# Up projection, quarters 1 to 3: both parts of h2 in one matmul of 512 columns

## The chip, the cores and the metric

The kernel runs on one core of one Trainium2 chip, in one launch. The metric is the device time of the kernel in microseconds (us). The kernel before takes 674.77 us, the median of 3 runs (674.47 to 674.83).

## What is computed

A decoder block on 512 tokens of width 1024 in float32. The part that the change touches is the MLP at its end:

```python
h2 = rmsnorm(x, norm_mlp_g[l])
z = jnp.square(jax.nn.relu(h2 @ w_up[l]))       # 1024 -> 4096
x = x + (z @ w_down[l]).astype(x.dtype)         # 4096 -> 1024
```

Ahead of it come a norm, one input projection, differential attention in 8 heads, a causal pooling in 4 groups, a gated merge and the output projection; after it, a final norm.

## The kernel before

Float32 products are made of three passes of the type fp32r: each operand x is split into a high part (a cast to fp32r) and a low part (x minus the high part), and high by high, high by low and low by high are added up in PSUM. The cast runs on ScalarE (`split_w`, L112), the subtraction on VectorE (L113).

The MLP goes in four quarters of 1024 hidden columns: `up(q)`, then `down(q)` (L975 to L979). Each is a multiplication of 2 by 2 blocks done with seven products in place of eight (Strassen's scheme in Winograd's form). The seven forms are named A11, A12, A22, S1, S2, S3, S4. For h2 they are made once, before quarter 0 (`forms_h2` and L655 to L662), and lie in the tiles `gab` and `gss` (L547 to L551): for each form the high part, then the low part, each of 4 k-tiles by 256 tokens (HS). Each quarter of w_up and of w_down has its seven forms made on the way by `weights` (L671): block b11 is loaded and cast; block sums are made by VectorE (L718) or by DMAs that add to what is in SBUF (L686, on POOL's queue); `parts` (L688) then splits each into wh and wl. Raw blocks b11 and b22 share two buffers (tag wr), b21 has one of its own, and wh and wl have room for three forms at a time, two in one pool and every third in another. The loads of raw blocks are on SP's queue (L681).

In `up`, `product` (L771) multiplies one form. Its output is 512 hidden rows (i = 0, 1 and p = 0, 1, 128 rows each) by 256 tokens. For one (i, p), it runs eight matmuls of 256 columns, high weights by the high (L782) and by the low part of h2 (L785), alternating over four k, and then four, low weights by the high part (L788): 12 matmuls. The two p of one i share a PSUM bank, so that a product has two banks of 512 columns. Twelve matmuls by four groups make 48 matmuls a product. `acc` hands out the banks 4, 5, 6, 7, 0, 1 in turn (L665); banks 2 and 3 (`m2`) belong to `down`.

In quarters 1 to 3, `up` goes in this order:

- A11 into the banks `ma`, copied to R[0] by ScalarE (`keep`, L810);
- S1 into the banks `mc`, copied to R[2];
- S2 onto `ma` (added in PSUM), copied to R[1];
- S3 onto `ma`, added to R[2] by VectorE (`join`, L814); ReLU and square of R[2] (`z_of`, L820, L821);
- A22 onto `ma`; ReLU straight out of the banks into R[3], and square;
- A12 into two banks of its own, joined to R[0] (`first_block`, L829), ReLU, square;
- S4 onto `mc`, joined to R[1].

From R, `sub` (L763, L765) makes the forms of z on VectorE and `zsplit` (L749) splits them (L752 ScalarE, L755 VectorE) for `down`. In `down`, the products (L865) have matmuls of 512 columns, in threes (L875, L877, L878), and VectorE adds the banks onto x1 (L895).

The order of the work on each engine is worked out when the kernel is built: a scheduler takes the instructions as their inputs come ready by its own estimate, and may put matmuls of one product between those of another. `after(later, earlier)` (L57) makes it place one instruction behind another; between two engines it adds no wait on the chip. The casts of the weights' forms are placed by such rules (`hold` in `parts`). Buffers and banks that are used again wait for their last reader.

Of the kernel before, what the change touches and what calls it, by code (L numbers as in the profile page):

```python
# [51 lines left out]
def block_kernel(ctx, tc, xT, x_tok, gains, pos, consts, w_in, w_v, w_pool, w_out, w_up, w_dn, out):  # L52
# [478 lines left out]
    HS = S // 2  # L531
# [12 lines left out]
    h2f = zf("h2f", F32)  # L544


    gab = [big.tile([P, j, 2, 4, HS], F32R, tag=t_, name=f"gab{j}") for j, t_ in ((1, "s1a"), (2, "s4"))]  # L547
    gss = [big.tile([P, 2, 2, 4, HS], F32R, tag=f"s{i}", name=f"gss{i}") for i in (2, 3)]
    gf = {}
    for form, g_, j in ((A11, gab[0], 0), (A12, gab[1], 0), (A22, gab[1], 1), (S1, gss[0], 0), (S2, gss[0], 1), (S3, gss[1], 0), (S4, gss[1], 1)):  # L550
        gf[form] = (g_[:, j, 0], g_[:, j, 1])  # L551
    rawz = bk.tile([P, 5, 4, HS], F32, name="rawz")
    R = [rawz[:, i] for i in range(5)]
    st = cp.tile([P, NT, 8], F32, name="st2")
# [36 lines left out]
    def forms_h2(forms, x):  # L591

        w, u, a11, a12 = (h_[:, i, :, x] for h_ in (hw, h2f) for i in range(2))
        for form in forms:
            ins = None
            if form in (S2, S4):
                ins = V.scalar_tensor_tensor(out=w, in0=w, scalar=-1.0, in1=a11 if form == S2 else a12, op0=ALU.mult, op1=ALU.subtract)
            elif form == S3:
                ins = V.tensor_tensor(out=u, in0=a11, in1=u, op=ALU.subtract)
            if form in (S3, S4):  # L600
                after(ins, state[form - 1])
            hi, lo = (g_[:, :, x] for g_ in gf[form])
            A.copy(out=hi, in_=u if form == S3 else w)
            state[form] = V.tensor_tensor(out=lo, in0=u if form == S3 else w, in1=f(hi), op=ALU.subtract)

# [20 lines left out]
    for t in range(NT):  # L626
        a_ = bank(4 + t, f"po1_{t}")
        for k in range(NK):
            m, end = mm_rows(a_, t, k, ws[k // 2], k == 0, k == NK - 1)
            if t > 1 and k == 0:  # L630
                after(m, state["po"])
        if 0 < t < 3:
            for b in range(2):
                after(state["h2T", t - 1, b], end)
        state["po"] = end
        x1_add(t, 1, a_)
        V.scalar_tensor_tensor(out=h2[:, t % 2], in0=x1[:, t, :], scalar=row_scale(t, 1), in1=g2b, op0=ALU.mult, op1=ALU.mult)
        pv = []
        for b in range(2):
            pt = bank((t % 2) * 2 + b, f"h2T{t}_{b}")  # L640
            for j in range(4):
                k = 4 * b + j
                if j == 1:
                    state["h2T", t, b] = state["h2T"]
                state["h2T"] = T.transpose(out=pt[:, j * P : j * P + P], in_=h2[:, t % 2, k * P : k * P + P], identity=ident)
            pv.append(pt.rearrange("p (j q) -> p j q", q=P))
        sl = slice((t % 2) * P, (t % 2) * P + P)
        if t > 1:

            A.copy(out=hw[:, 1, :, sl], in_=pv[0])  # L650
            V.tensor_tensor(out=hw[:, 0, :, sl], in0=pv[1], in1=hw[:, 1, :, sl], op=ALU.subtract)
            forms_h2((S1, S2), sl)
        if t == 3:
            forms_h2((S3,), slice(0, HS))
        for b in range(t // 2, 2):  # L655
            hi, lo = (gab[b][:, t // 2, i, :, sl] for i in range(2))
            A.copy(out=hi, in_=pv[b])
            part = V.tensor_tensor(out=lo, in0=pv[b], in1=f(hi), op=ALU.subtract)
            if t == 3:
                after(part, state[S3])  # L660
            if t < 2:
                A.copy(out=h2f[:, b, :, sl], in_=pv[b])  # L662
# [8 lines left out]
    def weights(src, q, nm, order):  # L671
# [16 lines left out]
        def parts(rs, b, hold=None, add=None):  # L688

            third = nparts[0] % 3 == 2  # L690
            nparts[0] += 1
            out_ = []
            for c in range(2):
                hi, lo = (
                    (bk if third else wp).tile([P, 1024], F32R, tag=t_ + "b" * third, name=f"{t_}_{nm}{b}_{q}_{c}", bufs=2 if third else 4)
                    for t_ in ("wh", "wl")
                )
                if add is None:
                    cast = split_w(rs[c], hi, lo, eng=V)
                else:  # L700

                    cast = A.copy(out=hi, in_=rs[c])
                    A.mul(out=lo, in_=f(hi), mul=-1.0)
                    G.dma_start(out=lo, in_=src[q, add, c], accum_op=ALU.add)
                if hold:
                    after(cast, hold)
                if early and b == f"t{A22}":
                    after(cast, state["keep"])
                out_.append((hi, lo))
            return out_  # L710

# [31 lines left out]
    def halves(r):  # L743
        return [r[:, 2 * i : 2 * i + 2, :] for i in range(2)]

    def bank_view(pa):
        return [pa[i].rearrange("p (a t) -> p a t", a=2) for i in range(2)]

    def zsplit(q, form, r):  # L749

# [16 lines left out]
    def up(q):  # L767

        W = weights(w_up, q, "u", (A11, A12, S1, S2, S3, A22, S4) if q == 0 else (A11, S1, S2, S3, A22, A12, S4))

        def product(form, name, onto=None):  # L771
            w, pa = next(W), onto or [acc(f"u{name}{q}_{i}") for i in range(2)]
            rh, rl = gf[form]
            first.append(None)
            for i in range(2):
                hi, lo = w[i]
                for p in range(2):
                    begin = None
                    a_ = pa[i][:, p * HS : p * HS + HS]
                    for k in range(4):  # L780
                        c = slice((p * 4 + k) * P, (p * 4 + k) * P + P)
                        m = T.matmul(a_, lhsT=hi[:, c], rhs=rh[:, k, :], start=p + k == 0 and onto is None, stop=False, skip_group_check=True)  # L782
                        first[-1] = first[-1] or m
                        begin = begin or m
                        T.matmul(a_, lhsT=hi[:, c], rhs=rl[:, k, :], start=False, stop=False, skip_group_check=True)  # L785
                    for k in range(4):
                        c = slice((p * 4 + k) * P, (p * 4 + k) * P + P)
                        m = T.matmul(a_, lhsT=lo[:, c], rhs=rh[:, k, :], start=False, stop=k == 3, skip_group_check=True)  # L788
                        if q == 0 and form == A12 and (i, p, k) == (1, 0, 0):
                            after(m, state["h2T"])  # L790
                    if q == 0:
                        if (form, i, p) == (A11, 0, 1):
                            for b in range(2):
                                after(state["h2T", 2, b], m)
                        elif (form, i, p) == (A11, 1, 1):
                            for b in range(2):
                                after(state["h2T", 3, b], m)
                        if form != A11 or i + p:
                            after(begin, state["um"])
                        state["um"] = m  # L800

            if form == A22:
                state["m4"] = m
            elif form == S4:
                after(first[-1], state["m4"])
            return pa

        def keep(pa, r):
            for a_, r_ in zip(bank_view(pa), halves(r)):
                state["keep"] = A.copy(out=r_, in_=a_)  # L810

        def join(pa, r, hold=None):
            for a_, r_ in zip(bank_view(pa), halves(r)):
                state["join"] = V.tensor_tensor(out=r_, in0=a_, in1=r_, op=ALU.add)  # L814
                if hold:
                    after(state["join"], hold)

        def z_of(r, sign, pa=None):
            for i, r_ in enumerate(halves(r)):
                A.activation(out=r_, in_=bank_view(pa)[i] if pa else r_, func=AF.Relu, scale=sign)  # L820
                ins = A.activation(out=r_, in_=r_, func=AF.Square)  # L821
            return ins

        ma = product(A11, "m1")
        keep(ma, R[0])
        if q == 0:
            forms_h2((S4,), slice(0, HS))
# [8 lines left out]
            first_block()  # L836
        mc = product(S1, "m5")
        keep(mc, R[2])
        product(S2, "m6", onto=ma)
        keep(ma, R[1])  # L840
        product(S3, "m7", onto=ma)
        join(ma, R[2])
        state["joined"] = state["join"]
        z_of(R[2], -1.0)
        product(A22, "m4", onto=ma)
        if q == 0:
            zsplit(q, A11, R[0])
        zhi["z21"] = z_of(R[3], 1.0, ma)
# [183 lines left out]
```

## Time and profile before

| what | value |
|---|---|
| median of 3 runs | 674.77 us (674.47 to 674.83) |
| the profiled execution's own time | 674.09 us |
| its span, first to last instruction | 671.9 us |
| around the span | 2.2 us |
| mean granted clock of TensorE | 0.996 |
| VectorE busy | 526.1 us (78%) |
| ScalarE busy | 461.0 us (69%) |
| up, quarters 1 to 3, with the down product that runs into it | 423.6 to 469.4, 502.1 to 547.9, 580.5 to 626.3 us |

PE is TensorE, PEld its weight loads, DVE VectorE, ACT ScalarE, POOL GpSimd, SP the engine whose queue issues most loads. A matmul's duration in the profile (283 ns at 256 columns, 389 ns at 512) is that of the whole pipeline; the time that one more matmul costs is the distance between the starts of two. A row of waits reads: who waited, for whom, us in total, times, longest. A row of the timeline reads: start and duration in us, engine, line, operation, output<-inputs, form, count, and in brackets how long the engine had been idle and what ended it. A row of a group reads: busy us, mean ns | idle us before it, and what ended that. A row of windows gives, for a stretch, the busy time (and count) of PE, PEld, DVE, ACT and POOL, the granted clock, the share of DMA and GB/s.

### The profile page before, as it was taken

The page shows a single profiled execution, that of the slowest core. Times are in us where ns is not written, and L with a number is a line of the kernel's source. Part 1 is how long each engine was busy: PE and PEld are TensorE (multiplying, and loading weights), DVE is VectorE, ACT ScalarE, POOL GpSimd, SP SyncE. Part 2 cuts the span into 40 slices and gives each one's busy share as a digit, 9 for nine tenths or more (in the row PEclk, how much of TensorE's full clock was granted, in tenths as well). Part 3 has the DMA queues.
Part 4 walks back from the last instruction along what each step waited for, and adds up shares of the span by engine and source line. Part 5 has one row for each costly group of instructions (what it writes and reads, how often), then busy time and mean ns, then how long its engine had stood idle before and what let it go on. Part 6 is the DMA issues. An engine that isn't in the chain of part 4 may idle for free.

```text
span 671.9 us, 9994 instructions
## 1 busy us (share of the span) xinstructions
PE 663.1 (99%) x3688; PEld 579.6 (86%) x3688; DVE 526.1 (78%) x882; ACT 461.0 (69%) x741; POOL 112.0 (17%) x130
## 2 busy tenths in 40 slices
PE   9999999999999999999999999999999999999995
PEld 7888888888888888888889988999889998899884
DVE  6855977799979986875588998657994599747995
ACT  8465587978887698884477975367743695256974
POOL 2001110142133212520202020202102021210120
PEclk9999999999999999999999999999999999999998
DMA  9416464435263365574976596776959578494863
GB/s 317 162 57 185 126 151 126 103 94 126 87 142 103 98 166 105 126 184 172 312 208 112 159 235 186 167 191 146 236 199 187 193 164 261 117 212 132 214 126 125
DMA packets 32880, 109.34 MB, mean 163 GB/s; under 512 B 4032, under 2 KB 4928, under 8 KB 32832
## 3 DMA queue, kind: packets, MB, share of 16 engines
q0 software_dynamic: 10656, 38.80, 32.3%
q1 hardware_dynamic: 21744, 69.38, 29.3%
q8 instruction: 29, 0.48, 0.3%
q10 hardware_dynamic: 432, 0.52, 0.2%
q14 instruction: 19, 0.16, 0.1%
HBM read 106.59 MB, written 2.10 MB: 162 GB/s over the span
## 4 chain that ended last, share of the span: by engine, by line
PE 98%; DMA 1%; DVE 0%; ACT 0%; issue 0%; SPq 0%
PE um L785 8%; PE um L788 8%; PE um L782 8%; PE dm L875 8%; PE dm L877 8%; PE dm L878 8%; PE v L235 2%; PE o L418 2%; PE ga L132 2%; PE ga L131 2%; PE gp L135 2%; PE gp L132 2%; PE k L132 2%; PE k L131 2%; PE gp L131 2%; PE k L135 2%
## 5 line engine op out<-in xcount | busy, mean ns | idle before, releaser
L877 PE MATMUL dm<-wh_dt,z 128*128 128x512 f32 (+1 forms) x128 | 49.5, 386 | 0.0
L878 PE MATMUL dm<-wl_dt,z 128*128 128x512 f32 (+1 forms) x128 | 49.4, 386 | 0.0
L875 PE MATMUL dm<-wh_dt,z 128*128 128x512 f32 (+1 forms) x128 | 49.0, 387 | 0.0
L785 PE MATMUL um<-gss,wh_ut 128*128 128x256 f32 x192 | 48.2, 283 | 0.0
L782 PE MATMUL um<-gss,wh_ut 128*128 128x256 f32 x192 | 48.0, 283 | 0.0
L401 ACT ACTIVATE p<-p,st 128x128 f32<-128x128 f32 (+3 forms) x64 | 35.7, 558 | 14.1 <-DVE st L397 13.8
L895 DVE TENSOR_TENSOR x<-x,dm 128x512 f32<-128x512 f32 x48 | 32.5, 681 | 16.3 <-PE dm L878 16.3
L112 ACT CAST wh_ut<-wga_uNone 128x1024 fp32r<-128x1024 f32 x24 | 24.9, 1050 | 29.7 <-PE dm L877 19.2
L112 ACT CAST wh_ub<-wr_u 128x1024 fp32r<-128x1024 f32 x24 | 25.1, 1050 | 22.1 <-PE um L785 9.8
L686 POOL DMA_DIRECT2D wga_dNone<-w_dn x16 | 14.2, 885 | 154.2 <-DVE wl_dt L113 154.2
L113 DVE TENSOR_TENSOR wl_ut<-wga_uNone,wh_ut 128x1024 fp32r<-128x1024 f32 x24 | 29.1, 1221 | 13.0 <-ACT wh_ut L112 12.9
L877 PE MATMUL dm<-wh_db,z 128*128 128x512 f32 x96 | 37.2, 389 | 0.0
L878 PE MATMUL dm<-wl_db,z 128*128 128x512 f32 x96 | 37.2, 389 | 0.0
L785 PEld LDWEIGHTS um<-gss,wh_ut 128*128 128x128 f32 x192 | 36.9, 192 | 0.0
L782 PEld LDWEIGHTS um<-gss,wh_ut 128*128 128x128 f32 x192 | 36.8, 192 | 0.0
L875 PE MATMUL dm<-wh_db,z 128*128 128x512 f32 x96 | 35.7, 389 | 0.0
L113 DVE TENSOR_TENSOR wl_ub<-wr_u,wh_ub 128x1024 fp32r<-128x1024 f32 x24 | 29.1, 1219 | 7.4 <-ACT wh_ub L112 7.4
L686 POOL DMA_DIRECT2D wga_uNone<-w_up x18 | 15.6, 865 | 115.8 <-DVE wl_ut L113 81.4
L112 ACT CAST wh_dt<-wga_dNone 128x1024 fp32r<-128x1024 f32 x24 | 24.9, 1049 | 14.4 <-issue 6.7
L755 DVE TENSOR_TENSOR z<-rawz,z 128x1024 fp32r<-128x1024 f32 x28 | 33.6, 1218 | 0.5 <-ACT z L752 0.5
L397 DVE CUSTOM_DVE_ANT_0 p<-s,mask 128x128 f32<-128x128 f32 (+3 forms) x64 | 30.3, 484 | 3.6 <-PE s L396 3.5
L785 PE MATMUL um<-gab,wh_ub 128*128 128x256 f32 x128 | 32.5, 283 | 0.0
(324 smaller groups left out, 2203.3 us busy)
## 6 DMA issues: line engine op xcount, KB each, us to landing
wr_u<-w_up SPq DMA_DIRECT2D x24, 512.0 KB, 5.4
wr_d<-w_dn SPq DMA_DIRECT2D x24, 512.0 KB, 4.2
wga_uNone<-w_up POOLq DMA_DIRECT2D x18, 512.0 KB, 7.2
wga_dNone<-w_dn POOLq DMA_DIRECT2D x16, 512.0 KB, 5.7
wr_k<-w_in SPq DMA_DIRECT2D x8, 512.0 KB, 3.3
wr_ga<-w_in SPq DMA_DIRECT2D x8, 512.0 KB, 3.3
wr_gp<-w_in SPq DMA_DIRECT2D x8, 512.0 KB, 4.2
wl_ga<-w_in POOLq DMA_DIRECT2D x8, 512.0 KB, 5.4
```

Of the source, the lines that this page charges most:

```text
L112: ins = A.copy(out=hi[:, sl], in_=raw[:, sl])
L113: (eng or G).tensor_tensor(out=lo[:, sl], in0=raw[:, sl], in1=f(hi)[:, sl], op=ALU.subtract)
L131: T.matmul(acc, lhsT=hi[:, c], rhs=rh[:, k, :], start=k == 0, stop=False)
L132: T.matmul(acc, lhsT=hi[:, c], rhs=rl[k], start=False, stop=False)
L401: A.activation(out=pr[:, c, :N], in_=pr[:, c, :N], func=AF.Exp, scale=-1.0, bias=st[:, c : c + 1], accum_out=st[:, 2 + c : 3 + c])
L755: lo = V.tensor_tensor(out=z[:, 1], in0=r, in1=f(z[:, 0]), op=ALU.subtract)
L782: m = T.matmul(a_, lhsT=hi[:, c], rhs=rh[:, k, :], start=p + k == 0 and onto is None, stop=False, skip_group_check=True)
L785: T.matmul(a_, lhsT=hi[:, c], rhs=rl[:, k, :], start=False, stop=False, skip_group_check=True)
L788: m = T.matmul(a_, lhsT=lo[:, c], rhs=rh[:, k, :], start=False, stop=k == 3, skip_group_check=True)
L875: m = T.matmul(a_, lhsT=zh, rhs=hi[:, sl], start=p == 0 and start, stop=False, skip_group_check=True)
L877: T.matmul(a_, lhsT=zl, rhs=hi[:, sl], start=False, stop=False, skip_group_check=True)
L878: end = T.matmul(a_, lhsT=zh, rhs=lo[:, sl], start=False, stop=p == 3, skip_group_check=True)
```

## The change

The tiles `gab` and `gss` are laid out so that, for each k, the high and the low part of h2 lie next to each other. In quarters 1 to 3 the products A11, S2, S3 and A22 are wide: each (i, p) has a bank of its own, and for each k one matmul of 512 columns streams both parts under the high weights, so that the first half of the bank gathers high by high and the second half high by low. The four low-weight matmuls of 256 columns go onto the first half. S1, S4 and A12 stay as they were, as does quarter 0.

`ma` then has four banks. Its two halves are added after the bank: `keep` copies the second half to R by ScalarE and VectorE adds the first; `join` adds both halves to R, one after the other, by VectorE; A22 goes through `keep` before its ReLU, which reads R. The banks are handed out by a list for each quarter: x and y to A11, z to S1, x again to A12, and in `down` y and x.

The casts of form A22 in quarters 1 to 3 are placed behind ScalarE's copies of S2's banks. In quarter 3 the second cast of A22 is placed behind S3's second join, those of block b21 (form A12) behind S3's sixth join and A22's first add, and those of b22 (form S4) behind A22's second add.

```diff
-    gab = [big.tile([P, j, 2, 4, HS], F32R, tag=t_, name=f"gab{j}") for j, t_ in ((1, "s1a"), (2, "s4"))]
-    gss = [big.tile([P, 2, 2, 4, HS], F32R, tag=f"s{i}", name=f"gss{i}") for i in (2, 3)]
+    gab = [big.tile([P, j, 4, 2, HS], F32R, tag=t_, name=f"gab{j}") for j, t_ in ((1, "s1a"), (2, "s4"))]
+    gss = [big.tile([P, 2, 4, 2, HS], F32R, tag=f"s{i}", name=f"gss{i}") for i in (2, 3)]
...
-        gf[form] = (g_[:, j, 0], g_[:, j, 1])
+        gf[form] = (g_[:, j, :, 0], g_[:, j, :, 1], g_[:, j])
...
-                if early and b == f"t{A22}":
-                    after(cast, state["keep"])
+                if b == f"t{A22}" and nm == "u":
+                    after(cast, state["keep"] if early else state["kept", 2 * c + 1])
+                if nm == "u" and q == 3:
+                    if b == f"t{A22}" and c == 1:
+                        after(cast, state["joins"][1])
+                    elif b == "b21":
+                        after(cast, state["added"][0] if c else state["joins"][5])
+                    elif b == "b22":
+                        after(cast, state["added"][1])
...
+    def split_view(b_):
+        return b_.rearrange("p (a t) -> p a t", a=2)
...
-        def product(form, name, onto=None):
-            w, pa = next(W), onto or [acc(f"u{name}{q}_{i}") for i in range(2)]
-            rh, rl = gf[form]
+        def product(form, name, onto=None, wide=False):
+            w, pa = next(W), onto or [acc(f"u{name}{q}_{i}") for i in range(4 if wide else 2)]
+            rh, rl, both = gf[form]
...
-                    a_ = pa[i][:, p * HS : p * HS + HS]
+                    if wide:
+                        ab = pa[2 * i + p]
+                        a_ = ab[:, :HS]
+                    else:
+                        a_ = pa[i][:, p * HS : p * HS + HS]
                     for k in range(4):
                         c = slice((p * 4 + k) * P, (p * 4 + k) * P + P)
+                        if wide:
+                            m = T.matmul(ab, lhsT=hi[:, c], rhs=both[:, k].rearrange("p a t -> p (a t)"), start=k == 0 and onto is None, stop=False, skip_group_check=True)
+                            first[-1] = first[-1] or m
+                            continue
...
         def keep(pa, r):
+            if len(pa) == 4:
+                state["added"] = []
+                for i, ab in enumerate(map(split_view, pa)):
+                    state["kept", i] = A.copy(out=r[:, i, :], in_=ab[:, 1])
+                    state["added"].append(V.tensor_tensor(out=r[:, i, :], in0=ab[:, 0], in1=r[:, i, :], op=ALU.add))
+                return
...
         def join(pa, r, hold=None):
+            if len(pa) == 4:
+                state["joins"] = []
+                for i, ab in enumerate(map(split_view, pa)):
+                    for j in range(2):
+                        state["joins"].append(V.tensor_tensor(out=r[:, i, :], in0=ab[:, j], in1=r[:, i, :], op=ALU.add))
+                return
...
         def z_of(r, sign, pa=None):
+            if pa and len(pa) == 4:
+                keep(pa, r)
+                pa = None
...
-        ma = product(A11, "m1")
+        wide = q > 0
+        if wide:
+            x, y, z = ((0, 1), (6, 7), (4, 5)) if q % 2 else ((4, 5), (6, 7), (0, 1))
+            acc.ids, acc.n = x + y + z + x + y + x + z, 0
+        ma = product(A11, "m1", wide=wide)
...
-        product(S2, "m6", onto=ma)
+        product(S2, "m6", onto=ma, wide=wide)
         keep(ma, R[1])
-        product(S3, "m7", onto=ma)
+        product(S3, "m7", onto=ma, wide=wide)
...
-        product(A22, "m4", onto=ma)
+        product(A22, "m4", onto=ma, wide=wide)
```

More of the change, by code (lines that the diff above doesn't have):

```diff
@@ L601, in forms_h2 @@
                 after(ins, state[form - 1])
-            hi, lo = (g_[:, :, x] for g_ in gf[form])
+            hi, lo = (g_[:, :, x] for g_ in gf[form][:2])
             A.copy(out=hi, in_=u if form == S3 else w)
@@ L655, in block_kernel @@
         for b in range(t // 2, 2):
-            hi, lo = (gab[b][:, t // 2, i, :, sl] for i in range(2))
+            hi, lo = (gab[b][:, t // 2, :, i, sl] for i in range(2))
             A.copy(out=hi, in_=pv[b])
@@ L744, in halves @@
         return [r[:, 2 * i : 2 * i + 2, :] for i in range(2)]
+    def split_view(b_):
+        return b_.rearrange("p (a t) -> p a t", a=2)
     def bank_view(pa):
-        return [pa[i].rearrange("p (a t) -> p a t", a=2) for i in range(2)]
+        return [split_view(pa[i]) for i in range(2)]
     def zsplit(q, form, r):
```

## The prediction

> **What bounds the kernel now.** I read the page first, then the waits of TensorE, then the chain of waits in two short windows for the pace of single matmuls, then VectorE and ScalarE by stretch, and last the timeline of the fourth quarter. The page:
>
> ```profile
> span 671.9 us, 9994 instructions
> PE 663.1 (99%) x3688; PEld 579.6 (86%) x3688; DVE 526.1 (78%) x882; ACT 461.0 (69%) x741; POOL 112.0 (17%) x130
> PE 98%; DMA 1%; DVE 0%; ACT 0%; issue 0%; SPq 0%
> ```
>
> The waits of TensorE over the whole run, all of them:
>
> ```profile
> PE warm L170 <- POOL eps L161: 1.1, 1, 1.1
> PE v L235 <- ACT wh_v L112: 0.5, 1, 0.5
> ```
>
> TensorE waits 1.6 us in all, before the first products; in the MLP it never waits. So time comes off only by giving TensorE less to do, and stays off only while VectorE, ScalarE and the loads keep ahead of it. The chain of waits in a window of the first up projection (start, us, piece), and in one of a down projection:
>
> ```profile
> 358.94 0.48 PE um L788 x4
> 359.42 0.12 PE um L782
> 359.54 0.12 PE um L785
> ...
> 360.38 0.48 PE um L788 x4
> ```
>
> ```profile
> 488.40 0.23 PE dm L878
> 488.63 0.68 PE dm L875 x3
> 489.31 0.23 PE dm L877
> ```
>
> A group of twelve 256-column matmuls, from one L788 piece to the next, takes 360.38 - 358.94 = 1.44 us: 120 ns each. Three 512-column matmuls take 0.68 us: 226.7 ns each, not 240. A second row, from the input projection, says the same (1.81 / 8 = 226 ns):
>
> ```profile
> 61.06 1.81 PE q L135 x8
> ```
>
> The 256 further columns cost 106.7 ns, so each matmul carries about 120 - 106.7 = 13.3 ns that do not depend on its width.
>
> **The change, part by part.** *TensorE.* In quarters 1 to 3 four of seven up products become wide: A11, S2, S3 and A22. A product has four groups (i, p). A group was 12 x 120 = 1440 ns. It becomes four 512-column matmuls with the high part of the weights, over both parts of h2, and four of 256 with the low part: 4 x 226.7 + 4 x 120 = 1387 ns, 53.3 ns less. With 3 x 4 x 4 = 48 groups that is 2.56 us; 192 matmuls and weight loads of 3688 go. No row has a 512-column um matmul or a 512 followed by a 256 in one group. The bounds are the two 256s it replaces (240 ns, gain nothing) and the dm row (226.7); I take the dm row, which has the same operand types and a new weight load at each matmul.
>
> The Trainium skill, "TensorE: Matmul & The Clock Gate", section "Wait — 56ns, not 53.3ns?", puts a warm matmul's fixed cost at about 2.5 ns, so that N columns take N / 2.4 GHz + 2.5 ns; an estimate from that page for the 192 matmuls saved is 0.48 us. The rows above disagree with it (13.3 ns), and the measurement decides.
>
> *Evacuation.* A wide bank holds the product with the high part of h2 in its first half and that with the low part in its second; they are added after the bank. Rows of before, by form:
>
> ```profile
> L814 DVE TENSOR_TENSOR rawz<-um,rawz 128x512 f32<-128x512 f32 x24 | 16.4, 685 | 7.3 <-PE um L788 7.3
> L935 DVE TENSOR_TENSOR x<-x,dm 128x256 f32<-128x256 f32 x1 | 0.4, 414 | 0.0
> L810 ACT COPY rawz<-um 128x512 f32<-128x512 f32 x24 | 14.0, 583 | 16.9 <-PE um L788 16.8
> L820 ACT ACTIVATE rawz<-um 128x512 f32<-128x512 f32 x8 | 4.7, 592 | 4.1 <-PE um L788 4.0
> L948 ACT ACTIVATE rawz<-x 128x256 f32<-128x256 f32 x2 | 0.8, 409 | 0.5 <-DVE x L945 0.5
> ```
>
> VectorE per quarter: A11, S2 and A22 gain four adds each (12 x 0.414 = 4.97 us); S3's join goes from two of 685 to eight of 414 ns (+1.94 us); together +6.9 us. ScalarE: a 256-column copy out of a bank has no row; it lies between half of L810 (0.29) and L948 (0.41). I take 0.37, nearer to L948, since halving columns does not halve these rows. Twelve copies are 4.4 us, less the four of 583 they replace: +2.1 us. A22's ReLU then reads SBUF, at about the same price. Busy time by stretch (columns PE, PEld, DVE, ACT, POOL):
>
> ```profile
> 502.00:513.00 11.00, 11.00 (x71) 9.98 (x71) 5.02 (x6) 3.75 (x4) 3.51 (x4) 1.00 0.89 188
> 513.00:524.00 11.00, 11.00 (x94) 11.00 (x94) 5.03 (x5) 5.99 (x8) 1.73 (x2) 1.00 0.97 226
> 524.00:538.00 14.00, 14.00 (x119) 14.00 (x118) 9.06 (x9) 9.32 (x13) 0.00 (x0) 1.00 0.48 163
> 603.00:617.00 14.00, 14.00 (x119) 14.00 (x118) 9.01 (x10) 9.85 (x13) 0.00 (x0) 1.00 0.45 159
> 617.00:626.00 9.00, 9.00 (x77) 9.00 (x77) 8.49 (x10) 7.53 (x11) 3.51 (x4) 1.00 0.60 119
> 626.00:649.00 23.00, 23.00 (x104) 19.09 (x104) 23.00 (x27) 20.93 (x26) 3.48 (x4) 1.00 0.86 186
> ```
>
> In quarter 2 VectorE idles 6.0 us in the stretch of A11, 6.0 in that of S1 and S2 and 4.9 in that of S3 and A22; A11's and S2's 1.66 us of adds each and the 3.6 us of S3 and A22 fit there. That idle time is the cover: without it the 6.9 us a quarter would stand behind TensorE. From 617 on VectorE has no room, so what slips past that point arrives late.
>
> *Banks.* S3 adds onto the banks that S2 left, so it waits for their copies and adds. Each bank ends a quarter product apart, 1.39 us, and is written again one product later, so copy and add have 3 x 1.39 = 4.16 us; they need 0.37 + 0.41 us and what stands ahead in two queues. For S3's join it is 0.83 us against the same 4.16. A12 now takes the first two banks of the wide four, so it cannot start before A22's are out. In before it filled in between the halves of S3:
>
> ```profile
> 607.96 0.28 PE L785 MATMUL um<-gab,wh_ub 128*128 128x256 f32 x1
> 608.08 0.28 PE L782 MATMUL um<-gss,wh_ut 128*128 128x256 f32 x1
> ```
>
> and the copy out of S2's second bank, on ScalarE:
>
> ```profile
> 605.46 0.58 ACT L810 COPY rawz<-um 128x512 f32<-128x512 f32 x1
> ```
>
> This filler goes. It covered little: the copy that S3's second half needs ended at 606.04, and sixteen A12 matmuls (1.92 us) brought TensorE to 608.08. What is late next is such a copy, held up behind weight casts on ScalarE; the change puts A22's casts behind the copies. I price this at nothing.
>
> *The fixed order of the last quarter.* The casts of A12 (b21) and S4 (b22) stand behind the joins and A22's adds. Behind them stand the second subtraction of each (VectorE), the release of the raw buffer, the loads of w_dn on SP's queue, and the add L718 that makes S1's down weights. VectorE, ending with the two z parts for down's A11 and A12, and where down's S1, A11 and A12 start on TensorE:
>
> ```profile
> 607.70 1.22 DVE L113 TENSOR_TENSOR wl_ub<-wr_u,wh_ub 128x1024 fp32r<-128x1024 f32 x1
> 611.77 1.22 DVE L113 TENSOR_TENSOR wl_ub<-wr_u,wh_ub 128x1024 fp32r<-128x1024 f32 x1
> 614.39 1.23 DVE L718 TENSOR_TENSOR wga_dNone<-wr_d,wal_d 128x1024 f32<-128x1024 f32 x1 [1.41 <-DMA wr_d<-w_dn]
> 616.65 1.23 DVE L718 TENSOR_TENSOR wga_dNone<-wr_d,wal_d 128x1024 f32<-128x1024 f32 x1 [1.04 <-DMA wr_d<-w_dn]
> 619.53 1.22 DVE L113 TENSOR_TENSOR wl_dt<-wga_dNone,wh_dt 128x1024 fp32r<-128x1024 f32 x1
> 628.74 1.22 DVE L755 TENSOR_TENSOR z<-rawz,z 128x1024 fp32r<-128x1024 f32 x1
> 634.48 2.35 DVE L755 TENSOR_TENSOR z<-rawz,z 128x1024 fp32r<-128x1024 f32 x2
> ```
>
> ```profile
> 626.32 0.63 PE L875 MATMUL dm<-wh_dt,z 128*128 128x512 f32 x2
> 631.78 0.62 PE L875 MATMUL dm<-wh_db,z 128*128 128x512 f32 x2
> 637.22 0.62 PE L875 MATMUL dm<-wh_db,z 128*128 128x512 f32 x2
> ```
>
> Count back from down's start, 626.32. S4 and A12 take 5.76 each, so A22 ends at 614.80 and its second bank at 612.02; copy and add make it 612.8. Two casts of 1.05 (row below) with two copies between end near 615.6, the last subtraction at 616.8 (in before at 612.99). The load then needs 616.65 - 612.99 = 3.66 us: 620.5. Add, cast and subtraction (1.22 + 1.05 + 1.22) end at 624.0.
>
> ```profile
> L112 ACT CAST wh_db<-wr_d 128x1024 fp32r<-128x1024 f32 x22 | 22.5, 1050 | 7.9 <-PE dm L877 5.9 <-DMA wr_d<-w_dn 1.0 <-PE um L785 1.0
> ```
>
> Needed at 626.32 plus six matmuls, 627.7: 3.7 us are left in place of 7.0 (619.53 + 1.22 = 620.75). But one or two L718 (1.13 us each at the pace of the rows) slip into the stretch where VectorE has no room, while z for A11 (ends 629.96) has 1.8 us to spare and z for A12 (first of the two, 635.7) 1.5 us. So 0 to 0.5 us may be lost here; below nothing it cannot go, as TensorE did not wait before. I take 0.2 us.
>
> *Rest.* Quarter 0 only reads and writes h2 at other strides, in runs no shorter than 128 elements; nothing. Quarters 1 and 2 have no fixed casts for b21 and b22.
>
> *Sum.* On the profiled execution's 674.09 us (span 671.9 and 2.2 around it): -2.56 + 0.2 = -2.36, so 671.7; from the median of 674.77, 672.4.
>
> **The rivals.** *B, VectorE late in quarter 3.* If both L718 wait for their load while the subtraction and z part behind them stand in the queue, the spare 1.5 us is overrun: two adds (2.3) and the two last adds of A22 (0.8), less 1.5 to spare, lose 1.6 us: 674.77 - 2.56 + 1.6 = 673.8. For it: L718 waited for a load in these rows already. Against: the loads may be issued in time for other work to go first.
>
> *C, slower.* One mechanism: L718 at the head of VectorE's queue, waiting for w_dn, in quarter 3. Behind the second one, done at 621.7, stand two joins (0.6 each at pace), two subtractions of weights (1.13 each), the difference R4 (1.13), its cast (1.05) and its low part (1.22): 628.6, 2.2 us after down's start. If that load takes as long as the first one did (608.92 to 614.39, 5.47 instead of 3.66) it is 4.0 us: 674.77 - 2.56 + 4.0 = 676.2. It decides from a wait of 2.56 us on. Against: it needs the worst order and the longer load.
>
> *D, the fixed cost doesn't go.* If the page's rule held for this pair of matmuls, or the low-part matmul after a wide one paid what the wide one saved, the gain would lie between 0 and 0.5 us: 674.3 to 674.8. The dm rows speak against.
>
> **How the numbers follow.** A measurement tells about 0.2% from no change, 1.35 us: faster is below 673.4, slower above 676.1. The forecast, 672.4 (its own range 671.9 to 673.0, the loss between 0 and 0.8), has 0.62; B 0.24 (673.0 to 674.6, a third of it below 673.4); D 0.05; C 0.09, of which 0.06 above 676.1. Faster: 0.62 + 0.08 = 0.70. Slower: 0.06. Same: the rest, 0.24. The range runs from 671.8, the full 2.56 and what medians scatter (0.3), to 674.6, the end of B.
>
> **What would show it.** Right: L788's line keeps 120 ns and the wide line shows 0.91 us for four; TensorE's waits stay near 1.6 us; 3496 matmuls; up in quarters 1 to 3 shorter by 0.85 us each. B or C: a TensorE wait on z or wl_dt of down in quarter 3, with VectorE's L718 waiting for wr_d before it. Wrong altogether: the wide matmuls at 240 ns, or TensorE waiting for the added adds (VectorE on um) inside up.

## The result and the profile after

The changed kernel takes 677.39 us, the median of 6 runs (676.88 to 680.44), against 674.62 us of the kernel before (6 runs, 673.77 to 674.87): a ratio of 1.0053, 95% interval 1.0041 to 1.0066. It is slower, by 2.8 us between the medians and 3.6 by the ratio; 672.4 us was forecast. The profiled execution took 677.23 us, 3.1 more than that of before. Its page, the rows that answer to those of before:

```profile
span 675.4 us, 9688 instructions
PE 662.8 (98%) x3496; PEld 568.7 (84%) x3496; DVE 544.0 (81%) x936; ACT 463.5 (69%) x765; POOL 112.1 (17%) x130
```

The 192 matmuls are gone (3688 to 3496), yet the span is 3.5 us longer. TensorE's waits, all of them (who waited, for whom, us, times, longest):

```profile
PE dm L915 <- DMA wl_db<-w_dn: 2.5, 1, 2.5
PE dm L915 <- DVE wl_dt L113: 1.2, 1, 1.2
PE warm L170 <- POOL eps L161: 1.1, 1, 1.1
PE v L235 <- ACT wh_v L112: 0.5, 1, 0.5
```

Two waits are new. Both are in `down` (L912, L914 and L915 are the matmuls that were L875, L877 and L878), both are for low parts of weights, and the timeline puts both in the last quarter:

```profile
629.66 0.61 PE L914 MATMUL dm<-wh_db,z 128*128 128x512 f32 x2
631.45 0.50 PE L915 MATMUL dm<-wl_dt,z 128*128 128x512 f32 x1 [1.18 <-DVE wl_dt L113]
631.79 0.39 PE L912 MATMUL dm<-wh_dt,z 128*128 128x512 f32 x1
...
650.63 0.39 PE L914 MATMUL dm<-wh_db,z 128*128 128x512 f32 x1
653.51 0.50 PE L915 MATMUL dm<-wl_db,z 128*128 128x512 f32 x1 [2.50 <-DMA wl_db<-w_dn]
653.85 0.40 PE L912 MATMUL dm<-wh_db,z 128*128 128x512 f32 x1
```

Read the distances between starts against the pace of 0.227: from the second of the two at 629.66 (629.89) to 631.45 is 1.56, so 1.34 us too long; from 650.63 to 653.51 is 2.88, so 2.66 too long; and the matmul behind each wait starts 0.34 after it, another 0.11 each. Together 4.2 us, more than the 3.7 us that the row of waits adds up to.

In a ledger of starts on TensorE: the first up matmul of quarter 1 comes 0.27 us later than in before (423.88, 423.61), the three up stages are shorter by 0.69, 0.53 and 0.69 (45.67 us each before), the stretches from there to the next up, of `down` in quarters 1 and 2, longer by 0.30 and 0.33, and the last one, to the start of the last matmul, longer by 4.54 (38.26 to 42.80). The sum is +3.5 us, the difference of the spans (675.4 and 671.9). So the gain of up is there, and the last `down` gives back more than all of it.

**The wide matmuls.** One quarter's S2 and S3, groups of four wide (L797) and four narrow (L806) matmuls:

```profile
521.51 1.08 PE L797 MATMUL um<-gss,wh_ut 128*128 128x512 f32 x4
522.43 0.64 PE L806 MATMUL um<-gss,wl_ut 128*128 128x256 f32 x4
522.90 1.09 PE L797 MATMUL um<-gss,wh_ut 128*128 128x512 f32 x4
...
528.51 1.09 PE L797 MATMUL um<-gss,wh_ut 128*128 128x512 f32 x4
```

The four wide take 0.92 us (0.91 forecast). Five groups from 521.51 to 528.51 take 1.40 us each; 1.387 was forecast, 1.44 is before. A quarter has 16 of them: 0.69 us saved, 43 ns a group instead of 53.3.

**The evacuation.** By form, the copies, adds and joins of the wide banks:

```profile
L831 DVE TENSOR_TENSOR rawz<-um,rawz 128x256 f32<-128x256 f32 x36 | 14.5, 418 | 2.4 <-ACT rawz L830 2.0
L830 ACT COPY rawz<-um 128x256 f32<-128x256 f32 x36 | 13.2, 371 | 10.9 <-PE um L806 10.6
L841 DVE TENSOR_TENSOR rawz<-um,rawz 128x256 f32<-128x256 f32 x24 | 9.3, 416 | 0.2
```

Adds at 418 and 416 ns (414 forecast) and copies at 371 (370) were well sized. What went wrong went wrong behind them.

**Where the last quarter is late.** VectorE in the changed kernel, from the low parts of b22 on:

```profile
613.95 2.36 DVE L113 TENSOR_TENSOR wl_ub<-wr_u,wh_ub 128x1024 fp32r<-128x1024 f32 x2
...
620.51 1.21 DVE L725 TENSOR_TENSOR wga_dNone<-wr_d,wal_d 128x1024 f32<-128x1024 f32 x1
622.17 1.23 DVE L725 TENSOR_TENSOR wga_dNone<-wr_d,wal_d 128x1024 f32<-128x1024 f32 x1 [0.44 <-DMA wr_d<-w_dn]
...
625.05 1.21 DVE L113 TENSOR_TENSOR wl_dt<-wga_dNone,wh_dt 128x1024 fp32r<-128x1024 f32 x1
626.18 1.22 DVE L773 SCALAR_TENSOR_TENSOR rawz<-rawz 128x1024 f32<-128x1024 f32 x1
627.31 1.22 DVE L765 TENSOR_TENSOR z<-rawz,z 128x1024 fp32r<-128x1024 f32 x1
628.45 0.68 DVE L844 TENSOR_TENSOR rawz<-um,rawz 128x512 f32<-128x512 f32 x1
629.05 1.21 DVE L113 TENSOR_TENSOR wl_db<-wr_d,wh_db 128x1024 fp32r<-128x1024 f32 x1
630.18 1.22 DVE L113 TENSOR_TENSOR wl_dt<-wga_dNone,wh_dt 128x1024 fp32r<-128x1024 f32 x1
```

L725 is the add that was L718, L773 and L765 the `sub` and the low part of z that were L763 and L755, L844 the narrow join. The two subtractions of b22 end at 616.3 (the first row; 612.99 in before). The adds L725 run from 620.51 and 622.17 (614.39 and 616.65 in before), 6.1 and 5.5 us later, though the second waited only 0.44 us for its load. The second low part of S1's down weights then stands behind a difference, a low part of z, a join and a subtraction, and ends at 631.40 instead of 620.75. That is TensorE's first wait.

The second comes a round of buffers later. SP's queue, first of before, then of the changed kernel (`x4`: two pairs of loads, starting with the first; `x2`: the pair for b22 of `down`, from which S4 is made):

```profile
607.21 6.12 SPq L681 DMA_DIRECT2D wr_d<-w_dn  x4
625.98 1.46 SPq L681 DMA_DIRECT2D wr_d<-w_dn  x2
```

```profile
613.37 3.29 SPq L681 DMA_DIRECT2D wr_d<-w_dn  x4
632.56 1.46 SPq L681 DMA_DIRECT2D wr_d<-w_dn  x2
```

The pair for S4 is issued 6.6 us later. In the last `down`, S4's low part is not made on VectorE: ScalarE writes the negated high part (L703) and a DMA on POOL's queue adds the raw weights to it from memory (L704). These DMAs, of before and of the changed kernel:

```profile
640.09 1.81 POOL L704 DMA_DIRECT2D wl_db<-w_dn  x2 [0.37 <-ACT wl_db L703]
```

```profile
641.10 0.86 POOL L704 DMA_DIRECT2D wl_db<-w_dn  x1 [6.76 <-ACT wl_db L703]
...
645.71 0.86 POOL L704 DMA_DIRECT2D wl_db<-w_dn  x1 [2.86 <-ACT wl_db L703]
```

The second left at 641.04 in before (inside the x2) and landed at 649.24; now it leaves at 645.71 and lands at 653.47, and TensorE starts at 653.51.

### The profile page after: what moved, and what is told of

Read it like the earlier page. It is cut to its first block, busy times and chain, and to the rows that moved or that the text cites. A ratio compares the mean times of both kernels' runs of the same rounds, so it can differ in the third digit from the quotient of the medians.

```text
span 675.4 us, 9688 instructions
## 1 busy us (share of the span) xinstructions
PE 662.8 (98%) x3496; PEld 568.7 (84%) x3496; DVE 544.0 (81%) x936; ACT 463.5 (69%) x765; POOL 112.1 (17%) x130
## 4 chain that ended last, share of the span: by engine, by line
PE 65%; issue 22%; DMA 10%; POOL 1%; DVE 1%; ACT 0%; SPq 0%; POOLq 0%
DMA wga_uNone<-w_up 5%; DMA wga_dNone<-w_dn 3%; PE dm L915 2%; PE dm L914 2%; PE dm L912 2%; PE um L806 2%; PE o L418 2%; PE ga L132 2%; PE ga L131 2%; PE gp L135 2%; PE gp L132 2%; PE k L132 2%; PE k L131 2%; PE gp L131 2%; PE k L135 2%
## 5 line engine op out<-in xcount | busy, mean ns | idle before, releaser
L915 PE MATMUL dm<-wl_dt,z 128*128 128x512 f32 (+1 forms) x128 | 48.8, 388 | 1.2 <-DVE wl_dt L113 1.2
L914 PE MATMUL dm<-wh_dt,z 128*128 128x512 f32 (+1 forms) x128 | 49.3, 386 | 0.0
L912 PE MATMUL dm<-wh_dt,z 128*128 128x512 f32 (+1 forms) x128 | 48.7, 387 | 0.0
L915 PE MATMUL dm<-wl_db,z 128*128 128x512 f32 x96 | 37.3, 391 | 2.5 <-DMA wl_db<-w_dn 2.5
L762 ACT CAST z<-rawz 128x1024 fp32r<-128x1024 f32 x28 | 28.3, 1046 | 14.3 <-DVE rawz L773 11.6
L914 PE MATMUL dm<-wh_db,z 128*128 128x512 f32 x96 | 37.5, 392 | 0.0
L113 DVE TENSOR_TENSOR wl_ut<-wga_uNone,wh_ut 128x1024 fp32r<-128x1024 f32 x24 | 29.0, 1220 | 9.7 <-ACT wh_ut L112 9.6
L912 PE MATMUL dm<-wh_db,z 128*128 128x512 f32 x96 | 35.8, 390 | 0.0
L765 DVE TENSOR_TENSOR z<-rawz,z 128x1024 fp32r<-128x1024 f32 x28 | 33.4, 1216 | 2.2 <-ACT z L762 2.2
L113 DVE TENSOR_TENSOR wl_ub<-wr_u,wh_ub 128x1024 fp32r<-128x1024 f32 x24 | 29.1, 1218 | 5.1 <-ACT wh_ub L112 5.0
L806 PE MATMUL um<-gss,wl_ut 128*128 128x256 f32 x192 | 30.5, 282 | 0.0
L113 DVE TENSOR_TENSOR wl_dt<-wga_dNone,wh_dt 128x1024 fp32r<-128x1024 f32 x24 | 29.1, 1217 | 1.3 <-ACT wh_dt L112 1.2
L915 PEld LDWEIGHTS dm<-wl_dt,z 128*128 128x128 f32 x128 | 24.0, 188 | 6.8 <-DVE wl_dt L113 1.9
L806 PEld LDWEIGHTS um<-gss,wl_ut 128*128 128x128 f32 x192 | 27.8, 190 | 2.0
```

The lines of the kernel that those rows point to most:

```text
L113: (eng or G).tensor_tensor(out=lo[:, sl], in0=raw[:, sl], in1=f(hi)[:, sl], op=ALU.subtract)
L765: lo = V.tensor_tensor(out=z[:, 1], in0=r, in1=f(z[:, 0]), op=ALU.subtract)
L912: m = T.matmul(a_, lhsT=zh, rhs=hi[:, sl], start=p == 0 and start, stop=False, skip_group_check=True)
L914: T.matmul(a_, lhsT=zl, rhs=hi[:, sl], start=False, stop=False, skip_group_check=True)
L915: end = T.matmul(a_, lhsT=zh, rhs=lo[:, sl], start=False, stop=p == 3, skip_group_check=True)
```

## The experiments

**Theories.** T1: the fixed order of the last quarter is the cause; it keeps the raw buffers of b21 and b22 too long. T2: the wide evacuation is the cause; 17.9 us more of VectorE (526.1 to 544.0) make it late whatever the order. Each experiment is compared with the kernel before on the same chip; ratios carry 95% intervals. By 'excess' I mean the sum, from the up projection of quarter 1 on, of how far the starts of matmuls are apart over a pace of 226.7 and 120 ns: 0.15 us in before, 6.0 in the changed kernel.

**1. No fixed order at all.** The changed kernel without its block for the last quarter:

```diff
-                if nm == "u" and q == 3:
-                    if b == f"t{A22}" and c == 1:
-                        after(cast, state["joins"][1])
-                    elif b == "b21":
-                        after(cast, state["added"][0] if c else state["joins"][5])
-                    elif b == "b22":
-                        after(cast, state["added"][1])
```

> The changed kernel without the fixed order of the last quarter's weight casts; all else stays, the twelve wide products too. Theory T1, the fixed order holds the casts of block b22 until A22's second bank is out, so the raw buffers come free late, w_dn's loads start late and TensorE waits in the last down projection: the 1.6 and 2.8 us of waits there go, TensorE waits for at most 0.5 us, about 677.4 - 4.4 = 673.0 us (ratio to before 0.9975). Theory T2, VectorE's 6.9 us of further adds a quarter make it late, whatever the order of ScalarE's casts: the waits stay or grow, 676.5 to 678 us (1.003 to 1.005).

675.21 us, ratio 1.0018 (1.0008 to 1.0028), between what the two theories gave. The last `down` has no wait on weights; instead up waits, in the last quarter's A22:

```profile
610.23 0.39 PE L800 MATMUL um<-gss,wh_ub 128*128 128x256 f32 x1 [0.55 <-ACT wh_ub L112]
...
612.42 0.96 PE L797 MATMUL um<-gab,wh_ut 128*128 128x512 f32 x3 [0.98 <-DVE rawz L841]
```

Without the holds, VectorE has a subtraction of weights (1.22 us) between most of the joins (0.42) of S3, and A22 can't be added onto a bank that isn't joined yet. So the order had a use: it moved a wait of about 2 us out of up, and put 4 us into `down`.

**2. Only b22 freed.**

```diff
-                    elif b == "b22":
-                        after(cast, state["added"][1])
```

> The changed kernel with the fixed order kept for A22's second cast and for block b21, and taken away for block b22 alone. T1 with b22 as the cause: nearly all comes back, 673.0 to 673.8 us. T1 with b21 (one buffer of its own) or A22 as the cause: 676 to 677.4. T2: no change, 676.5 to 678.

672.50 us, ratio 0.9970 (0.9959 to 0.9981): some 5 us faster than the changed kernel (profiled 672.61 against 677.23), and faster than before. Without these two lines of the seven the loss is gone. TensorE's waits, beside that at the very start:

```profile
PE um L797 <- DVE rawz L841: 0.4, 1, 0.4
```

and SP's and POOL's queues, close to the times of before again:

```profile
609.19 7.33 SPq L681 DMA_DIRECT2D wr_d<-w_dn  x4
...
626.13 2.06 SPq L681 DMA_DIRECT2D wr_d<-w_dn  x2
```

```profile
639.54 2.11 POOL L704 DMA_DIRECT2D wl_db<-w_dn  x2
```

With b22 free and b21 held, the scheduler puts b22's casts first: its subtractions end at 609.16 and 611.29 (616.3 in the changed kernel), the first pair on SP's queue goes into its buffers, and the adds L725 run at 613.34 and 615.61.

**3. Only b22 held.** The changed kernel with the hold of b22 and without those of A22 and b21:

```diff
                 if nm == "u" and q == 3:
-                    if b == f"t{A22}" and c == 1:
-                        after(cast, state["joins"][1])
-                    elif b == "b21":
-                        after(cast, state["added"][0] if c else state["joins"][5])
-                    elif b == "b22":
+                    if b == "b22":
                         after(cast, state["added"][1])
```

> The changed kernel with the fixed order for block b22 alone; A22's second cast and b21 are free. Theory T1', two effects: b22's hold costs what the last down projection waits for (raw buffer freed late, w_dn late), and the holds of A22 and b21 keep VectorE free for S3's joins, without which A22 waits in up. Then this has both losses, at least the 677.4 us of the changed kernel: 677 to 679.5. Rival: b22's hold only hurts together with b21's, as the casts then crowd together; then about the 675.2 us of the run without any order.

675.47 us, ratio 1.0016 (1.0007 to 1.0025): the two losses did not add up, as the theory had it. Here A22 waits in up as in experiment 1, and the last `down` for a low part of z, but neither for weights of S1 nor for those of S4 (S4's second DMA lands at 651.81, not 653.47):

```profile
PE um L797 <- DVE rawz L841: 1.6, 1, 1.6
...
PE dm L914 <- DVE z L765: 1.1, 1, 1.1
```

That the hold of b22 is harmless alone is not shown by this. S4's second DMA still lands 2.6 us later than in before (649.24), but TensorE, held up in up and by z, comes to the matmul that needs it only at 652.92; in the changed kernel it was ready for it at 650.86. So a part of what the hold costs may be hidden behind the other waits.

**4. The order without wide products.** The kernel before with the same holds, behind the nearest instructions that it has (S3's joins; for b21's second cast and both of b22, A22's first ReLU):

```diff
-                if early and b == f"t{A22}":
-                    after(cast, state["keep"])
+                if nm == "u" and (early and b == f"t{A22}" or q == 3 and (b in ("b21", "b22") or b == f"t{A22}" and c)):
+                    after(cast, state["keep"] if early else state["join", 0] if b == f"t{A22}" else state["join", 1] if b == "b21" and not c else state["relu", 0])
```

> The kernel before, all products narrow and no further adds, with only the fixed order put in for the last quarter: A22's second cast behind S3's first join, b21 behind S3's second join and A22's first ReLU, b22 behind A22's first ReLU. T1: TensorE waits in the last down projection as in the changed kernel, up to 4.4 us: 677 to 679 us (1.003 to 1.0065). T2: the order alone does no harm, 674.4 to 675.0 (within 0.1% of before).

681.21 us, ratio 1.0096 (1.0082 to 1.0109): the order alone, with no wide matmul and no added VectorE work, costs some 7 us. That the order is the cause, T1, is shown. The wait is S4's again:

```profile
651.26 0.39 PE L875 MATMUL dm<-wh_db,z 128*128 128x512 f32 x1
656.00 0.80 PE L878 MATMUL dm<-wl_db,z 128*128 128x512 f32 x1 [4.35 <-DMA wl_db<-w_dn]
656.59 0.63 PE L875 MATMUL dm<-wh_db,z 128*128 128x512 f32 x1
657.02 0.63 PE L877 MATMUL dm<-wh_db,z 128*128 128x512 f32 x1
```

It is longer than in the changed kernel (651.26 to 656.00: 4.5 us too long, against 2.66), although POOL issues its second L704 at nearly the same time (646.12 and 645.71): here two other adding DMAs went out between S4's two, where the changed kernel has one. In both kernels these DMAs land in the order of their issue, 2.5 us apart (648.48, 650.94, 653.43 and 655.96 here), so S4's second landed 9.8 us after its issue instead of 7.8. And the matmuls behind the wait are 0.43 us apart, of which more below.

On S1's weights TensorE loses only 0.36 us here, where the changed kernel lost 1.45. Yet their second low part is just as late: it ends at 631.28 (631.40 in the changed kernel). The difference is TensorE, which begins the last `down` at 626.37 here and at 625.30 there. So the order makes these weights late with or without the added VectorE work, and the first wait takes back what the wide matmuls had gained.

**5. The same without b22.** `b in ("b21", "b22")` of experiment 4 becomes `b == "b21"`.

> The kernel before (narrow), with the fixed order of the last quarter for A22's second cast and for b21 alone, nothing for b22. T1 (the holds hurt the last down only where b21 and b22 are both held, as with wide products): no TensorE wait above 0.4 us in the last down, 674 to 675.5 us against 674.4. T2 (b21's hold is enough where the products are narrow, because it shifts everything behind it on VectorE): a wait of S4 for wl_db of 1 us or more, 676 or more. The order with b22 had 681.2.

674.56 us, ratio 1.0004 (0.9994 to 1.0013); no wait in the last `down`, excess 0.25 us. With the narrow products, too, the loss goes when b22 is freed; whether the hold of b22 would cause it alone was not run.

**6. S4's weights split by VectorE.** The changed kernel, where S4's low part in the last `down` is made by a subtraction (L113) as elsewhere, not by the negated copy and the adding DMA:

```diff
-                yield parts(raw(3), "b22", None, 3 if nm == "d" and q == 3 else None)
+                yield parts(raw(3), "b22", None, None)
```

> The changed kernel, but the low part of the last down projection's S4 weights is made by VectorE's subtraction, as in the other quarters, in place of a negated copy on ScalarE and an adding load on POOL's queue. T1: the wait of 2.8 us on that load goes or shrinks to under 1 us, as the raw block is there by then, the earlier wait of 1.5 us stays: 674.6 to 675.5 us. T2: 2.4 us more on a late VectorE delay z, and the time stays at 677 us or above.

675.79 us, ratio 1.0018 (1.0009 to 1.0026). The wait on the DMA is gone; those on S1's weights stay, and there are two now:

```profile
PE dm L915 <- DVE wl_dt L113: 2.1, 2, 1.2
```

So the two waits are separate effects of one delay, and this change removes only the second; freeing b22 (experiment 2) removes both.

**7. VectorE's load alone.** The kernel before with 17 idle passes of 256 columns a quarter on VectorE in up (the maximum of a tile with itself), about what the wide evacuation adds:

```diff
-        keep(ma, R[0])
+        keep(ma, R[0]); again(R[0], 4)
```

and the like behind S2's copies (4), S3's joins (5) and A22's ReLU (4), with

```diff
+        def again(r, n):
+            for i in range(n if q else 0): V.tensor_tensor(out=r[:, i % 4, :], in0=r[:, i % 4, :], in1=r[:, i % 4, :], op=ALU.max)
```

> The kernel before, narrow throughout, with seventeen further 256-column passes a quarter on VectorE in quarters 1 to 3 (each the maximum of a tile with itself, which changes nothing) where the wide products add theirs: 17 x 0.41 = 7 us a quarter. T2, the load on VectorE alone makes TensorE wait: 676 us or more, with waits on z and wl in down. T1': VectorE's idle time takes most of it, TensorE waits under 0.8 us in all: 674.2 to 675.0.

675.75 us, ratio 1.0021 (1.0011 to 1.0031), between what the two theories gave. The 51 passes take 418 ns each, and VectorE is busy for 543.5 us, as in the changed kernel (544.0). In the profiled execution, which at 674.77 us was among the faster ones, it is mostly one wait in the last up:

```profile
PE um L782 <- ACT wh_ub L112: 0.7, 1, 0.7
```

T2 is not nothing: the load alone costs about 1.4 us where no order moves the casts. But, as far as that execution shows, it costs it in up; S4 in the last `down` loses 0.24 us.

**8. The holds of A22 and b21 in quarter 2 too.** Experiment 2 with `q > 1` for `q == 3`.

> The run with b22 freed, with the same holds of A22's second cast and of b21 put into quarter 2 as well. T1': quarter 2's wait of A22 on S3's joins (0.2 to 0.7 us over the runs) goes, the rest stays: 671.9 to 672.4 us. Rival: holding b21's casts crowds VectorE later, before down, as much as it frees it: 672.5 or more.

672.31 us, ratio 0.9970 (0.9960 to 0.9980); profiled 671.78 us. A22's wait in quarter 2 is gone and the excess is 0.92 us, the least of the wide kernels. Its time can't be told from experiment 2's; both beat both kernels.

**9. Wide and narrow in turn.** Experiment 2, each wide matmul followed by its k's low-weight one, where there are four and four:

```diff
                             first[-1] = first[-1] or m
-                            continue
+                            m = T.matmul(a_, lhsT=lo[:, c], rhs=rh[:, k, :], start=False, stop=k == 3, skip_group_check=True); continue
...
-                    for k in range(4):
+                    for k in range(0 if wide else 4):
```

> The run with b22 freed, with the wide products' matmuls in another order: for each k the 512-column matmul, then at once the 256-column one with the low weights, in place of four and four. P1, a 256-column matmul costs 120 ns because a weight load takes that long, while its columns need 113 (the first ones after a wide matmul show 112 to 117): next to a 512 the load is hidden, a pair costs 226.5 + 113 = 340 ns, a group 1359 in place of the measured 1402: 48 x 43 = 2.1 us faster than the 672.5 of the run with b22 freed, 670.4 us. P2, each matmul carries 13.3 ns and each change of width costs some 15 ns more: 48 x 3 further changes x 15 = 2.2 us slower, 674.7.

674.70 us, ratio 1.0004 (0.9995 to 1.0013). One pair and the start of the next:

```profile
525.62 0.40 PE L797 MATMUL um<-gss,wh_ut 128*128 128x512 f32 x1
525.86 0.28 PE L799 MATMUL um<-gss,wl_ut 128*128 128x256 f32 x1
525.97 0.40 PE L797 MATMUL um<-gss,wh_ut 128*128 128x512 f32 x1
```

A pair takes 0.35 us; over some 170 pairs the mean from wide to narrow is 235.6 ns and from narrow to wide 116.8, 352 a pair and 1.41 us a group. That is 48 x 9 ns = 0.4 us more than four and four, where P2 had 2.2. So P1, a gain, falls, and P2's time of 674.7 came out by luck: the rest of the 2.2 us by which this kernel is behind experiment 2 is waits that came with the other order, 1.7 us of them for the two parts of z in `down` of quarter 1.

**10. Eight and eight.** Experiment 8 with the low-weight matmuls of both p of one i behind the eight wide ones:

```diff
-                    for k in range(4):
+                    for k in range((8 * p) if wide else 4):
...
```

> The best version so far (order without b22, in quarters 2 and 3; 672.3 us) with the two groups of one i taken together: eight matmuls of 512 columns, then eight of 256, in place of four and four twice. P1 (a change of width costs, some 17 ns for each 512 to 256 and back): 24 changes fewer, two groups take 2790 in place of 2804 ns, 0.35 us less in sum, about 672.0 us. P2 (the 512s are slower for themselves near narrow ones): the intervals 512 to 512 stay near 232 ns and the time at 672.3. The intervals between the starts tell them apart; the time hardly can. A wait that appears because banks end in pairs would show as a wait on um or rawz and speak for neither.

672.74 us, ratio 0.9976 (0.9966 to 0.9986), with a loss of 0.7 us at an add in quarter 1, so the time speaks for neither theory. The scheduler kept about a third of the eights whole. In those, the fifth wide matmul still takes 231 ns, the sixth to eighth 226.7, with narrow ones before and behind the eight: the price lies at the change of width.

**Together**, ratios to the kernel before:

| holds in the last quarter | narrow products | wide products |
|---|---|---|
| none | 1 | 1.0018 |
| A22, b21 | 1.0004 | 0.9970 |
| b22 | not run | 1.0016 |
| A22, b21, b22 | 1.0096 | 1.0053 |

## Why the prediction was wrong

**The failed step** is "The fixed order of the last quarter ... 3.7 us are left in place of 7.0 ... I take 0.2 us". It cost some 5 us (changed kernel against experiment 2, where only the hold of b22 is gone). Three things were missing in it.

First, the count back from TensorE's start was right to within a microsecond at its beginning (last subtraction of b22 at 616.8; measured 616.3) and wrong behind it. The load came in at 622.07, not 620.5: four loads leave SP's queue between 613.37 and 616.66 and overlap, where in before they were spread over 6.1 us, so that the last took 5.7 us and not 3.66. The forecast took its price from a load that had the queue nearly to itself.

Second, from the landed load to the end of the last subtraction it counted three operations at their own durations, 3.5 us. They took 9.3 (622.07 to 631.40), because ScalarE casts a part of z and of b11's weights in between, and VectorE has four other instructions ahead of the last. The list is close to the one of rival C, which put the two joins, weight subtractions and R4 behind a waiting L718; but C's cause, an L718 that blocks VectorE, is not what happened: it waited 0.44 us. C's consequence came through a full queue, not through a stalled one.

Third, the forecast followed the release of the raw buffers to S1's weights only. They are used once more in the same `down`: b11's low part ends late, so S4's loads leave at 632.56, and behind them come a cast, a negated copy and a DMA on POOL's queue that takes 7.8 us (8.2 in before). That was 2.8 of the 4.2 us, with the late matmul behind the wait, and no part of the sum.

**The wide matmuls** were right in mechanism and sized a bit high: 43 ns a group, 0.69 us a stage where nothing waits or 2.07 for the three, not 2.56. The term that was mis-sized is 4 x 226.7 + 4 x 120 = 1387 ns, which took both paces from long runs of one width: in the changed kernel the four wide matmuls take 928 ns, not 907, and the four narrow ones 473, not 480, together 1401. The Trainium skill, "TensorE: Matmul & The Clock Gate", section "Wait — 56ns, not 53.3ns?", with its 2.5 ns of fixed cost gave an estimate of 0.48 us; by the ledger above this kernel disagrees. Rival D, a gain of 0.5 us at most, falls by the same ledger.

**The filler in up** was priced "at nothing", which was wrong where nothing is held: experiments 1 and 3 lose about 2 us to A22 that waits for S3's joins. That the filler would have covered this is not shown; the trace shows the subtractions between the joins, which the forecast's 0.83 us for a join left out. The holds of A22 and b21 repair it, and with them alone 672.5 and 672.3 us are measured. That the forecast was 672.4 is partly luck: the gain of the wide matmuls was smaller, and the kernel before was faster in that comparison (674.2 and 674.4, not 674.77); by the ratio 2.0 us are gained, not 2.36. Rival B's place, VectorE late in quarter 3, was right, its size was not. (The lower end of the range adds up to 671.9, not 671.8.)

**Open** is why both holds together cost far more than the sum of the two: the traces show the order that comes out (b22's subtractions ahead of b21's where b21 is held and b22 is free, behind them in every other kernel here, and both late where both are held), not the scheduler's estimates behind it. The narrow kernel with b22 alone was not run.

## What to carry to other kernels

When a change holds a cast back, follow the buffer it frees through every later use in the stage, not only the next: here the second use, with a DMA of 7.8 us at its end, cost twice what the first did. Count the way from a landed load to a matmul with what stands between in each in-order queue, at the loads' spacing after the change, not with the bare durations. And free or hold one block at a time: with five of the seven lines of order the kernel is 2 us faster than before, with all seven 3.6 us slower.

## What the runs showed of the hardware

After the long wait of experiment 4 TensorE ran at half pace. Windows of that kernel, and of the changed one around its 2.9 us (columns as before: PE, PEld, DVE, ACT, POOL, granted clock, DMA):

```profile
651.00:656.00 5.00, 0.65 (x3) 0.19 (x2) 5.00 (x9) 2.78 (x5) 0.00 (x0) 0.84 0.78 155
656.00:661.00 5.00, 5.00 (x12) 3.94 (x13) 2.16 (x3) 1.42 (x5) 0.00 (x0) 0.50 0.01 3
```

```profile
650.60:653.50 2.90, 0.42 (x2) 0.00 (x0) 2.90 (x6) 1.83 (x5) 0.00 (x0) 1.00 1.05 209
653.50:658.00 4.50, 4.49 (x20) 3.70 (x21) 3.90 (x7) 1.92 (x4) 0.00 (x0) 1.00 0.23 45
```

After a gap of 4.7 us between starts, the clock stood at 0.50, and the matmuls from 656.59 on started 427 instead of 227 ns apart until 660.86: the twelve distances from 656.00 to 661.27 add up to 2.5 us more than at pace. After a gap of 2.9 us the clock stayed at 1.00. The Trainium skill, "TensorE: Matmul & The Clock Gate", section "Part 1: The HAM clock gate", has the clock fall to half after an idle window of about 3.4 us; the two rows lie on either side of it. But no fixed length of wait follows from the traces. In experiment 4 the clock fell at 654.41, 3.15 us after the last start, and it came back at 661.24. At the ends of the twelve kernels it fell between 2.2 and 5.5 us after the last matmul's start (2.26 in before, 5.19 in the changed kernel), and each stretch of full clock before a fall lasted a whole multiple of 3.41 us. So whether a wait of two to five us costs the half clock too depended on where it lay; here, a wait that grew from 2.7 to 4.5 us cost not 1.8 but 4.3 us more.

Two smaller things. In the traces here, a matmul of 512 columns behind a wait of 0.16 to 2.7 us is followed 107 to 114 ns late at full clock, whatever the length of the wait (but for one of 0.31 us near the end of experiment 6: 79 ns). And among 256s, the first four 512s take 234, 234, 231 and 229 ns (means over some 36 in the changed kernel) where long runs have 226.7, while the narrow ones behind them take 117 to 119 for 120: a change of width and back costs some 14 ns.
